# A one-layer hybrid decoder step on one core: where the sampled tokens' state steps stand among the products, and two calls of the output projection's decode rows made one

## The chip, the cores and the metric

The kernel runs on one core of a Trainium2 chip. The metric is the device time of one execution in microseconds (us); three executions of the kernel before took 915.9, 916.09 and 916.25 us, median 916.09 us. The engines are called as in the profile: PE (matrix engine), PEld (its weight loads), DVE (vector), ACT (scalar), POOL and SP (here mostly issuers of DMAs).

## The reference, cut to what matters

One layer of a decoder that joins an RG-LRU group and an mLSTM group of heads. There are two sets of tokens: a prompt of 1,024 new positions, and 8 sampled sequences with one new token each, which carry a state of their own ("decode").

```python
hn = rmsnorm(x, g_norm)
u = hn @ w_in                                    # 1024 -> 7176
xa, za, uq, uk, uv, uo, zb, ui, uf = jnp.split(u, SPLIT_IDX, axis=-1)
yA, hA, bufA = rglru_branch(xa, ...)
hB, C, n, m = mlstm_seq(q, k, v, ig, lf, C0, n0, m0)   # 4 heads, DK = DV = 256
merged = concat([yA * silu(za), norm(sigmoid(uo) * hB) * g * silu(zb)])   # 2048 wide
x = x + merged @ w_out                           # 2048 -> 1024
# inside mlstm_seq, for a sampled token (chunk length 1):
num   = P @ v + ginter * (q @ C)
C_new = carry_scale * C + decay * k v^T          # 256 x 256, per sequence and head
```

For the 8 sampled tokens and 4 heads that is 32 matrices `C` of 256 x 256 floats, which are read, scaled, given a rank-one update, written back and multiplied by a query.

## The kernel before, in words

**The products of the input projection.** `w_in` is taken in 15 *units* of two 256-column blocks each (`UNITS`: v0v1, x0y0, q0k0, ..., z2z3). A unit is worked as 7 products (`Q_P1` to `Q_P7`, in the order `RQ`), each of half the size in every dimension, with sums of operands ahead and sums of results behind. A product has two halves, so a unit has 14 *parts*. A half is a run of triples of full 128x128 matmuls on PE (`mm3`, L66 to L68: high times high, low times high, high times low), 24 of them per half, into one accumulator. What PE reads is split into a high and a low piece first, by ACT (L72) and DVE (L73). DVE takes finished halves out of the accumulators (`evac`, L325 to L362).

**The decode rows of a unit.** The 8 sampled tokens go through the same block of `w_in` in `dec_unit` (L249 to L270): 8 matmuls with a stationary tile of only 32 columns (L256), four side by side in the array. `preps` emits it just behind a unit's last part, so it stands between two units' products on PE. Four transposes (L264) turn the result later.

**The decode steps.** `decode_steps(h)` (L973 to L1028) gives the state steps of head `h`. `first` makes the scaled key and the query tiles and fetches the value row of token 0 (`fetch_v`, L965, an SP queue's DMA into `vbc`). `token(b)` scales the loaded state `Cb` on ACT (L992), adds the rank-one update on DVE (two instructions, L994), stores the state (L996), fetches the next value row and, for even tokens, two more states (`fetch_C`, L971; four buffers `Cb`). For each odd token `products` (L1013) follows two pops later on the list `late`: a *burst* of 4 matmuls with a stationary tile of 4 columns (32 for a head's first burst), 256 wide, over the two states just made. There are 16 bursts in all. The first burst of a head reads `qfirst`, the others `qsel`.

**What sets their places.** Behind every part of a product the main loop (L1690 on) calls `pop_bg` (L712): first it runs what is on `late`, then one entry each of three queues: `bg` (single steps), `rgq` (the RG-LRU group) and `dcq` (the decode steps). `dcq` is popped only on some parts: `DEC = 10, 2, 3` says every third part in units below 10 and every second from unit 10. `first` is a step of its own, so a head has 9 steps. Within an engine a scheduler then moves instructions by its own estimate of when operands are ready.

**From the products to the output.** In the last unit `wo_due` (L1645) loads blocks of `w_out` and makes sums of them (L1379) for a second such set of products, the half of the output projection that belongs to the RG-LRU group. `dec_block` (L1359) multiplies the sampled tokens' rows by those blocks: 8 matmuls of 32 columns for each of two calls (L1368). From there on the tail loop (L1737) takes the prompt's mLSTM chunks and out-projection products in turn. The rows 8 to 15 of `w_out` (the mLSTM group's half) meet the sampled tokens in `wo_dec` (L1483, matmuls L1490 with 32 columns), in two calls: four rows at tail step 19 and four at step 21. Each call ends in `dec_put` (L1353): an ACT copy out of the accumulator and a store that adds into memory.

Of the kernel before, what the change touches and what calls it, by code (L numbers as in the profile page):

```python
# [20 lines left out]
NB = 8  # L21
# [21 lines left out]

UNITS = "v0v1 x0y0 q0k0 x1y1 q1k1 x2y2 v2v3 q2k2 x3y3 q3k3 o0o1 o2o3 z0z1 z2z3".split()
NWS, NSTG, LEAD = 6, 7, 2
DEC = 10, 2, 3
RQ = [Q_P1, Q_P2, Q_P5, Q_P6, Q_P7, Q_P4, Q_P3]
NR, NZ = 28, 4

# [2 lines left out]
def hymba_kernel(  # L52
# [7 lines left out]
    V, A, G, TE = nc.vector, nc.scalar, nc.gpsimd, nc.tensor  # L60
# [21 lines left out]
    def ps(tag, shape):  # L82
        return psp.tile(shape, F32, tag=tag, name=f"ps_{tag}", bufs=NBUF.get(tag, 1))
# [136 lines left out]
    late = []  # L220
    lastt = []

    def run_late():
        now = late[:]
        late.clear()
        for f in now:
            f()
# [482 lines left out]

    bg, rgq, dcq = deque(), deque(), deque()

    def pop_bg(n=1, rg=1, dc=1):
        run_late()
        for q, m in ((bg, n), (rgq, rg), (dcq, dc)):
            for _ in range(m):
                if q:
                    q.popleft()()


    fpr = {}
# [251 lines left out]
    def decode_steps(h):  # L973

        p2 = fpr["p"]
        qsel, qfirst, selq = fpr["qsel"], fpr["qfirst"], fpr["selq"]
        st = {}

        def first():
            st["kw"] = kw = p2.tile([P, 2, NB], F32, tag="kw", name="kw")  # L980
            V.tensor_tensor(kw, dk[:, 2 * h:2 * h + 2, :], dW[:, :, h].unsqueeze(1).to_broadcast([P, 2, NB]), op=ALU.mult)
            V.tensor_copy(qsel.rearrange("p k (m r) -> p k m r", r=9)[:, :, :, 0:5:4],
                          dq[:, 2 * h:2 * h + 2, :].rearrange("p k (m r) -> p k m r", r=2))
            V.tensor_copy(qfirst[:, :, :, 0], dq[:, 2 * h:2 * h + 2, 0:2])
            fetch_v(h, 0)

        def token(b):
            i = h * NB + b

            def f():  # L990
                vb_, C = ds_.pop(("v", i)), ds_["C", i]
                A.mul(C, C, dGI[:, b, h:h + 1])  # L992
                for kb in range(2):
                    V.scalar_tensor_tensor(C[:, kb, :], vb_, st["kw"][:, kb, b:b + 1], C[:, kb, :],  # L994
                                           op0=ALU.mult, op1=ALU.add)
                stq(s_C[0, b, h].rearrange("(kb p) v -> p kb v", p=P), C)  # L996
                if b + 1 < NB:
                    fetch_v(h, b + 1)
                if b % 2:
                    late.append(lambda: late.append(products))  # L1000
                else:
                    fetch_C(i + 2)
                    fetch_C(i + 3)


            def products():
                if b == 1:
                    st["pq"] = ps("qp", [P, 512])
                pq = st["pq"]
                for g in range(4):  # L1010
                    bb, kb = b - 1 + g // 2, g % 2
                    q, n = (qfirst[:, kb, bb, :], 32) if b == 1 else (qsel[:, kb, 4 * bb:4 * bb + 4], 4)
                    TE.matmul(pq[32 * g:32 * g + n, 0:256], q, ds_["C", h * NB + bb][:, kb, :], start=b == 1,  # L1013
                              stop=b == NB - 1, skip_group_check=True)
                for bb in (b - 1, b):
                    del ds_["C", h * NB + bb]
                if b == NB - 1:
                    Z = sg([P, 256], "qC")
                    V.tensor_copy(Z, pq[:, 0:256])

                    def turn():
                        pt = pq[:, 256:272].rearrange("p (v b) -> p v b", v=2)
                        for vb in range(2):
                            TE.matmul(pt[:, vb, :], Z[:, vb * P:(vb + 1) * P], selq, start=True, stop=True)
                        V.tensor_copy(dqC[:, 2 * h:2 * h + 2, :], pt)
                    late.append(lambda: late.append(turn))
            return f
        return [first] + [token(b) for b in range(NB)]  # L1028


    def bh(t):
# [304 lines left out]
    oraw = {}  # L1336
# [145 lines left out]
    def wo_dec(ms):  # L1482

        po = ps("tr", [P, 512])
        with tc.manual_schedule(engines={mybir.EngineType.PE}):
            for m in ms:
                md = mAd[:, NB * (m % 8):NB * (m % 8) + 32]
                for half in range(2):
                    g = 2 * (m % 2) + half
                    TE.matmul(po[32 * g:32 * g + 32, :], md, oraw[m][:, half * 512:(half + 1) * 512], start=m < ms[2],  # L1490
                              stop=m >= ms[2], skip_group_check=True)
        dec_put(po, accum_op=ALU.add)

    def wo_split(**at):
# [34 lines left out]
    def tail():  # L1529
        while tails:  # L1530
            tails.pop(0)()
# [114 lines left out]
    def wo_due(q):  # L1646

        step = lambda *ns: bg.extend([lambda n=n: w_step(n) for n in ns])
        if q == 0:
            w_slot(0, 0, 0)  # L1650
            w_slot(1, 0, 1)
        elif q == 1:
            w_slot(1, 1, 2)
        elif q == 2:
            bg.append(lambda: dec_block(0))
            step("s3", Q_P1)
        elif q == 3:
            bg.append(lambda: dec_block(1))
            step("s1", "s2", "s4")
        elif q == 4:  # L1660
            step(Q_P2)
            bg.append(m_open3)
            step(Q_P5)
        elif q == 5:
            step(Q_P6)
            bg.append(lambda: (r_op(0), r_op(1), r_two()))
            step(Q_P7)
# [12 lines left out]
    last_u = len(units) - 1  # L1680
# [10 lines left out]
    part = 0  # L1691
    for n, (u, q) in enumerate(seq):
        preps(n + 1 + LEAD)
        for _ in product(u, q):
            pop_bg(2 if u == 1 or u == last_u else 1, 1, part % DEC[1 if u >= DEC[0] else 2] == 1)
            part += 1
        if u == last_u:
            wo_due(q)
        if q == 6:
            for kind, j in units[u]:  # L1700
                if kind == "x":
                    rg_unit(j)
            for half in range(2):
                if u == max(unit_of["v", 2 * half], unit_of["v", 2 * half + 1], 1):
                    bg.append(lambda half=half: dec_rows(half))
            for h in range(NH):
                if done_h[h] == u:
                    bg.append(lambda h=h: dcq.extend(decode_steps(h)))
            if u == last_u - 1:
                dgen = decode_outputs()  # L1710

                def step():
                    next(dgen, None)
                    run_late()
                state["out"] = [step] * 5 + [m_open2]
        if not state["m"] and u > max(done_h) and not (bg or rgq or dcq or late):
            m_start()
        if u == last_u and q == 0:
            if not state["m"]:
                while bg or rgq or dcq or late:  # L1720
                    pop_bg()
                m_start()
            bg.extend(state["out"])
# [10 lines left out]
    N2 = 18  # L1734
    for n in range(4, N):
        c, h = n // 4, n % 4
        m_a(n)  # L1737
        so_load(n)
        if n > 4:
            m_g(n - 1)  # L1740
            if n > N2 + 3:
                next(dend, None)
        if n == 6:
            mx["gf"] = gf = [sg([P, HT], f"gf{m}") for m in range(2)]
            for m in range(2):
                stq(gf[m], g_final[m * HT:(m + 1) * HT].partition_broadcast(P))
        m_load(n + 2)
        if h == 3 or n == 4:
            z_load(c if h == 3 else 0)
        if h == 0:  # L1750
            m_n(c - 1)
            fill(2 if n < N2 else 1)
            m_k(n + 1)
            fill(1)
            m_b(n)
            fill(1)
        elif h == 1:
            m_zg(c - 1)
            if n == N2 + 3:
                wo_dec((12, 13, 14, 15))  # L1760
            fill(1)
            m_k(n + 1)
            fill(1)
            m_z(c - 1, 0)
            m_b(n)
            fill(1)
            m_z(c - 1, 1)
            if c - 1 == NZ - 1:
                z_back(NZ - 1)
            elif c - 1 >= NZ:  # L1770
                work.extend([out_part(c - 1, half) for half in range(2)])
            fill(n < N2)
        else:
            fill(1)
            if n == N2 + 1:
                wo_dec((8, 9, 10, 11))
            tail()
            m_k(n + 1)
            fill(2 if n < N2 or h == 2 else 1)
            m_b(n)  # L1780
            fill(1)
# [47 lines left out]
```

## Time and profile before

| what | us |
|---|---|
| median of three executions | 916.09 |
| lowest, highest | 915.9, 916.25 |
| span of the profiled execution | 913.5 |
| PE busy | 902.1 (99%) |
| DVE busy | 741.5 (81%) |
| ACT busy | 590.1 (65%) |
| POOL busy | 194.2 (21%) |

The span is what the profiler saw between the first and the last instruction of one execution. It is 2.6 us less than the median of the executions without a profiler; what lies around the span is taken as unchanged below. Busy shares are means over the span. A matmul's row in the timeline gives its start and the time until its result is out; consecutive matmuls overlap, so the distance from start to start is what one costs.

### The profile page before, as it was taken

Reading aid. Unit: us, or ns where it says so; the run is one execution under the profiler, and the core shown is the slowest. Engines: PE = TensorE matmul, PEld = TensorE weight load, DVE = VectorE, ACT = ScalarE, POOL = GpSimd, SP = SyncE. Lnnn points to the kernel's source line nnn. Section 1 sums busy time; section 2 is a strip of 40 time slices with the busy share of each in tenths; the row PEclk is TensorE's granted clock in tenths of the full one; section 3 lists DMA queues with packets and bytes.
Section 4 is the critical chain, followed back from the end, with each engine's and each line's share of the span. In section 5 each row is a group of like instructions: output and inputs, shape, how many; then the busy total and the mean of one; then the engine's idle time right before and its main releaser. Section 6 shows DMA issues by size and latency. Waiting matters only on the chain.

```text
span 913.5 us, 15513 instructions
## 1 busy us (share of the span) xinstructions
PE 902.1 (99%) x5259; PEld 749.2 (82%) x5259; DVE 741.5 (81%) x1532; ACT 590.1 (65%) x1086; POOL 194.2 (21%) x322
## 2 busy tenths in 40 slices
PE   8999999999999999999999999999999999999996
PEld 6897777877787988787789898877788888888886
DVE  6874788978689878789888786679998879888973
ACT  7663446867567776577658786446786568566642
POOL 1111113112312222324332334010111111121120
PEclk9999999999999999999999999999999999999999
DMA  6611457455746566548665747345789889846531
GB/s 202 193 62 46 138 170 243 134 201 186 229 152 212 165 198 198 192 144 265 202 237 167 266 139 243 108 132 188 217 230 260 201 206 300 225 138 183 181 123 68
DMA packets 130488, 167.68 MB, mean 184 GB/s; under 512 B 17596, under 2 KB 98564, under 8 KB 130402
## 3 DMA queue, kind: packets, MB, share of 16 engines
q1 hardware_dynamic: 108790, 103.68, 37.4%
q0 software_dynamic: 21616, 63.02, 21.0%
q8 instruction: 41, 0.67, 0.3%
q14 instruction: 37, 0.30, 0.1%
q10 hardware_dynamic: 4, 0.00, 0.0%
HBM read 108.00 MB, written 62.92 MB: 187 GB/s over the span
## 4 chain that ended last, share of the span: by engine, by line
PE 97%; ACT 1%; DVE 1%; DMA 0%; issue 0%; POOL 0%; ACTq 0%; POOLq 0%
PE ps_o L66 16%; PE ps_o L68 15%; PE ps_o L67 15%; PE ps_kv L66 12%; PE ps_kv L68 11%; PE ps_kv L67 11%; PE ps_o L256 2%; PE ps_s L1195 2%; PE ps_qp L1013 1%; PE ps_s L824 1%; PE ps_tr L824 1%; PE ps_qp L67 1%; PE ps_qp L66 1%; PE ps_qp L68 1%; PE ps_s L1197 1%; PE ps_o L264 1%
## 5 line engine op out<-in xcount | busy, mean ns | idle before, releaser
L72 ACT CAST wh<-raw 128x1024 fp32r<-128x1024 f32 x91 | 95.4, 1049 | 77.9 <-PE ps_o L67 19.3
L73 DVE TENSOR_TENSOR wl<-raw,wh 128x1024 fp32r<-128x1024 f32 x91 | 111.0, 1220 | 34.9 <-ACT wh L72 19.8
L66 PE MATMUL ps_kv<-cb_hi,wh 128*128 128x512 f32 x320 | 127.3, 398 | 0.0
L68 PE MATMUL ps_kv<-cb_hi,wl 128*128 128x512 f32 x320 | 125.3, 392 | 0.0
L67 PE MATMUL ps_kv<-cb_lo,wh 128*128 128x512 f32 x320 | 125.0, 391 | 0.0
L66 PE MATMUL ps_o<-cb_hi,wh 128*128 128x512 f32 x240 | 95.2, 397 | 0.0
L68 PE MATMUL ps_o<-cb_hi,wl 128*128 128x512 f32 x240 | 93.7, 391 | 0.0
L67 PE MATMUL ps_o<-cb_lo,wh 128*128 128x512 f32 x240 | 93.6, 390 | 0.0
L66 PEld LDWEIGHTS ps_kv<-cb_hi,wh 128*128 128x128 f32 x320 | 60.1, 188 | 22.3 <-issue 4.6
L68 PEld LDWEIGHTS ps_kv<-cb_hi,wl 128*128 128x128 f32 x320 | 60.1, 188 | 13.0
L67 PEld LDWEIGHTS ps_kv<-cb_lo,wh 128*128 128x128 f32 x320 | 60.1, 188 | 12.7 <-issue 0.8
L66 PE MATMUL ps_kv<-wh,cb_hi 128*128 128x256 f32 x192 | 55.1, 287 | 0.0
L67 PE MATMUL ps_kv<-wl,cb_hi 128*128 128x256 f32 x192 | 54.4, 283 | 0.0
L68 PE MATMUL ps_kv<-wh,cb_lo 128*128 128x256 f32 x192 | 54.3, 283 | 0.0
L68 PEld LDWEIGHTS ps_o<-cb_hi,wl 128*128 128x128 f32 x240 | 45.1, 188 | 9.9
L66 PEld LDWEIGHTS ps_o<-cb_hi,wh 128*128 128x128 f32 x240 | 45.1, 188 | 9.7 <-issue 0.8
L66 PE MATMUL ps_o<-wo,mh 128*128 128x512 f32 (+1 forms) x136 | 53.0, 390 | 0.0
L67 PEld LDWEIGHTS ps_o<-cb_lo,wh 128*128 128x128 f32 x240 | 45.2, 188 | 8.9
L68 PE MATMUL ps_o<-wo,ml 128*128 128x512 f32 (+1 forms) x136 | 51.7, 380 | 0.0
L67 PE MATMUL ps_o<-wo,mh 128*128 128x512 f32 (+1 forms) x136 | 51.5, 379 | 0.0
L66 PE MATMUL ps_o<-wh,cb_hi 128*128 128x256 f32 x144 | 41.0, 285 | 0.0
L67 PE MATMUL ps_o<-wl,cb_hi 128*128 128x256 f32 x144 | 40.7, 283 | 0.0
(560 smaller groups left out, 2599.8 us busy)
## 6 DMA issues: line engine op xcount, KB each, us to landing
raw<-in_w_in_dram SPq DMA_DIRECT2D x55, 512.0 KB
Cb<-in_state_mlstm_C_dram SPq DMA_DIRECT2D x32, 256.0 KB
out_dram<-Cb POOLq DMA_DIRECT2D x32, 256.0 KB, 4.5
qk<-d_qk SPq DMA_DIRECT2D x32, 256.0 KB
ring<-d_ro SPq DMA_DIRECT2D x26, 256.0 KB
d_qk<-s POOLq DMA_DIRECT2D x24, 256.0 KB, 4.9
d_x<-s POOLq DMA_DIRECT2D x16, 256.0 KB, 2.8
zsr<-d_y SPq DMA_DIRECT2D x16, 256.0 KB
```

Source lines behind the costliest of these rows:

```text
L66: TE.matmul(out, ah, bh, start=first, stop=False, skip_group_check=True)
L67: TE.matmul(out, ah, bl, start=False, stop=False, skip_group_check=True)
L68: TE.matmul(out, al, bh, start=False, stop=last, skip_group_check=True)
L72: a = A.copy(hi, src)
L73: V.tensor_tensor(lo, src, hi.bitcast(F32), op=ALU.subtract)
L256: TE.matmul(pz[32 * g:32 * g + 32, :], hnd[:, NB * k:NB * k + 32], raws[u, k // 4][:, k % 4, :], start=k < 4, stop=k >= 4, skip_group_chec ...
L264: TE.transpose(pt[:, m, :], Z[:, m * P:(m + 1) * P], idF)
L824: TE.matmul(pg, w[:, n, :], st["xx"][n], start=k == 0, stop=k == 1)
L1013: TE.matmul(pq[32 * g:32 * g + n, 0:256], q, ds_["C", h * NB + bb][:, kb, :], start=b == 1, stop=b == NB - 1, skip_group_check=True)
L1195: TE.matmul(S, qk[:, 2 + kb, :], qk[:, kb, :], start=kb == 0, stop=kb == 1)
L1197: TE.transpose(kn[:, kb * P:(kb + 1) * P], qk[:, 2 + kb, :], idF)
```

## The change

1. `DEC` becomes four places in a unit's 14 parts: decode steps are popped behind parts 2, 5, 8 and 11, in all units.
2. `pop_bg` takes what is on `late` first, and with `late_last` runs it behind the queues' entries instead of ahead of them. The main loop sets that at part 13, the last of a unit, so that a burst due there is emitted directly ahead of the next unit's decode rows.
3. `first` and `token(0)` become one step, so a head has 8 steps, two units' worth.
4. `dec_block(0)` and `dec_block(1)` become one entry of `bg`.
5. `wo_dec` handles rows 8 to 15 in one call at tail step 21, with one `dec_put`.

```diff
-DEC = 10, 2, 3
+DEC = 2, 5, 8, 11
...
-    def pop_bg(n=1, rg=1, dc=1):
-        run_late()
+    def pop_bg(n=1, rg=1, dc=1, late_last=False):
+        now = late[:]
+        late.clear()
+        if not late_last:
+            for f in now:
+                f()
         for q, m in ((bg, n), (rgq, rg), (dcq, dc)):
             for _ in range(m):
                 if q:
                     q.popleft()()
+        if late_last:
+            for f in now:
+                f()
...
-        return [first] + [token(b) for b in range(NB)]
+        start = token(0)
+        return [lambda: (first(), start())] + [token(b) for b in range(1, NB)]
...
-                    TE.matmul(po[32 * g:32 * g + 32, :], md, oraw[m][:, half * 512:(half + 1) * 512], start=m < ms[2],
-                              stop=m >= ms[2], skip_group_check=True)
+                    TE.matmul(po[32 * g:32 * g + 32, :], md, oraw[m][:, half * 512:(half + 1) * 512], start=m < 10,
+                              stop=m >= 14, skip_group_check=True)
...
-            bg.append(lambda: dec_block(0))
             step("s3", Q_P1)
         elif q == 3:
-            bg.append(lambda: dec_block(1))
+            bg.append(lambda: (dec_block(0), dec_block(1)))
...
-            pop_bg(2 if u == 1 or u == last_u else 1, 1, part % DEC[1 if u >= DEC[0] else 2] == 1)
+            pop_bg(2 if u == 1 or u == last_u else 1, 1, part % 14 in DEC, part % 14 == 13)
...
-                wo_dec((12, 13, 14, 15))
+                wo_dec(range(8, 16))
...
-            if n == N2 + 1:
-                wo_dec((8, 9, 10, 11))
```

The lines after L712 move down by 7 or 8, so the burst L1013 is L1020 in the changed kernel, L1368 is L1376, L1379 is L1387, L1490 is L1498.

Three places show how the instructions move. The first is PE at the end of a unit, where the decode rows `L256` stand between one unit's last triples and the next unit's first. Before, the burst comes four triples behind them, among triples of the next unit's first product:

```order
L67 MATMUL ps_kv<-cb_lo_188,wh_0_2118 128x512
L68 MATMUL ps_kv<-cb_hi_187,wl_0_2119 128x512
L1013 MATMUL ps_qp<-Cb,qsel 4x256 x4
L66 MATMUL ps_kv<-cb_hi_187,wh_0_2118 128x512
L67 MATMUL ps_kv<-cb_lo_188,wh_0_2118 128x512
```

and in the changed kernel at the same end of a unit:

```order
L68 MATMUL ps_kv<-cb_hi_199,wl_6_2059 128x512
L1020 MATMUL ps_qp<-Cb,qsel 4x256 x4
L256 MATMUL ps_o<-raw_4_1943,hnd 32x512 x4
L256 MATMUL ps_o<-raw_4_2062,hnd 32x512 x4
L66 MATMUL ps_kv<-cb_hi_187,wh_0_2118 128x512
L67 MATMUL ps_kv<-cb_lo_188,wh_0_2118 128x512
```

The burst has moved up against the decode rows. That is so for 8 of the 16 bursts, each head's second and fourth; the other 8 still stand alone among triples.

The second place is DVE at the hand-over from the last unit to the output projection. `s<-s,ps_kv` (L343) takes a half of the last unit's fifth product out of the accumulator, `ws` (L1379) are sums of blocks of `w_out`, `wr1l` the low piece of one of the operands of the next products. Before:

```order
L1379 TENSOR_TENSOR ws_6801<-wc_6632,ws_6717 128x1024
L343 TENSOR_TENSOR s_6651<-s_6651,ps_kv 128x512
L1379 TENSOR_TENSOR ws_6804<-wc_6658,ws_6801 128x1024
L362 SCALAR_TENSOR_TENSOR s_6651<-tz,s_6651 128x512
L1372 COPY mAd<-mBd 128x64
L1379 TENSOR_TENSOR ws_6804<-wc_6658,ws_6801 128x1024
L73 TENSOR_TENSOR wr1l<-wc_6658,wr1h 128x1024
L343 TENSOR_TENSOR s_6685<-s_6685,ps_kv 128x512
L73 TENSOR_TENSOR wr1l<-wc_6658,wr1h 128x1024
```

and in the changed kernel, where `s_6685` is called `s_6666`:

```order
L1387 TENSOR_TENSOR ws_6781<-wc_6521,wc_6612 128x1024
L343 TENSOR_TENSOR s_6666<-s_6666,ps_kv 128x512
L1387 TENSOR_TENSOR ws_6801<-wc_6612,ws_6705 128x1024 x2
L1387 TENSOR_TENSOR ws_6804<-wc_6673,ws_6801 128x1024
L1380 COPY mAd<-mBd 128x64
L1387 TENSOR_TENSOR ws_6804<-wc_6673,ws_6801 128x1024
L362 SCALAR_TENSOR_TENSOR s_6666<-tz,s_6666 128x512
L347 TENSOR_TENSOR s_6703<-s_6703,ps_o 128x512
L73 TENSOR_TENSOR wr1l<-wc_6673,wr1h 128x1024
```

The two passes each of `ws_6801` and `ws_6804`, the copy and the first pass of `wr1l` stood ahead of this half's evacuation and now stand behind it.

The third place is PE where the sampled tokens' rows meet `w_out` in the last unit (`dec_block`). In the changed kernel the second call stands here:

```order
L68 MATMUL ps_o<-cb_hi_197,wl_5_6688 128x512
L66 MATMUL ps_o<-cb_hi_197,wh_5_6687 128x512
L1376 MATMUL ps_tr<-wc_6673,mAd 32x512
L1376 MATMUL ps_tr<-wc_6612,mAd 32x512
L1376 MATMUL ps_tr<-wc_6673,mAd 32x512
L1376 MATMUL ps_tr<-wc_6612,mAd 32x512
```

Although both calls are one entry of the queue, the scheduler leaves 19 full matmuls between the two runs of 8, and the second run now stands behind the end of the half in `ps_kv`, where before it stood inside that half. In the tail all 16 matmuls of `wo_dec` (L1498) stand in one run, where before there were two runs of 8 (L1490).

## The prediction

> **What bounds the kernel now.** I read the page first, for who is busy and for the chain of waits; then PE's waits; then PE's timeline around a burst, since nearly all of the change is about where small matmuls stand; and last the windows at the hand-over from the last unit to the output projection, where the order changes most.
>
> ```profile
> PE 902.1 (99%) x5259; PEld 749.2 (82%) x5259; DVE 741.5 (81%) x1532; ACT 590.1 (65%) x1086; POOL 194.2 (21%) x322
> PE 97%; ACT 1%; DVE 1%; DMA 0%; issue 0%; POOL 0%; ACTq 0%; POOLq 0%
> ```
>
> PE works 902.1 of 913.5 us, and 97% of the chain that ended last is PE. What PE waits for, by the view of its waits, whose two largest rows these are (us in total, times, longest):
>
> ```profile
> PE ps_tr L533 <- POOL ones L116: 1.1, 1, 1.1
> PE ps_o L67 <- DVE w1l L73: 0.9, 1, 0.9
> ```
>
> No row of that view names a burst, a decode step or a state's DMA. So the time is PE's own sequence, and the change is worth what it takes out of that sequence, unless a place where another engine is about to be late gives it back. The windows show one:
>
> ```profile
> 617.00:640.00 23.00, 22.93 (x117) 17.09 (x116) 22.54 (x57) 14.96 (x23) 2.15 (x4) 1.00 0.56 193
> 640.00:660.00 20.00, 20.00 (x96) 15.16 (x95) 19.56 (x27) 15.38 (x24) 2.74 (x5) 1.00 0.72 217
> 660.00:690.00 30.00, 29.31 (x164) 24.82 (x163) 28.74 (x65) 24.43 (x53) 6.78 (x10) 1.00 0.80 225
> ```
>
> The columns are the length, then busy PE, PEld, DVE, ACT and POOL, the granted clock (1.00) and the DMA share. Over the whole span DVE is 81% busy; here it works 22.54 of 23, 19.56 of 20 and 28.74 of 30 us. PE is the bound in this stretch only just: whatever makes PE earlier here meets a DVE that has nothing left.
>
> **The bursts beside the decode rows.** The cost of a burst that stands alone, from PE's timeline (start, time to the result):
>
> ```profile
> 206.33 0.39 PE L67 MATMUL ps_kv<-cb_lo,wh 128*128 128x512 f32 x1
> 206.56 0.39 PE L68 MATMUL ps_kv<-cb_hi,wl 128*128 128x512 f32 x1
> 206.88 0.61 PE L1013 MATMUL ps_qp<-Cb,qsel 128*4 128x256 f32 x8
> 207.43 0.50 PE L66 MATMUL ps_kv<-cb_hi,wh 128*128 128x512 f32 x1
> 207.76 0.39 PE L67 MATMUL ps_kv<-cb_lo,wh 128*128 128x512 f32 x1
> ```
>
> Full matmuls start 0.23 us apart (206.33, 206.56). The burst starts 0.32 behind the last of them, 0.09 more than the pitch: the entry. The first matmul behind it takes 0.33 to the next, 0.10 more: the exit. From 206.56 to 207.76 are 1.20 us, of which two pitches are 0.46, so the burst costs 0.74. The decode rows by the same reading:
>
> ```profile
> 201.72 0.39 PE L68 MATMUL ps_kv<-cb_hi,wl 128*128 128x512 f32 x1
> 202.04 1.92 PE L256 MATMUL ps_o<-raw,hnd 128*32 128x512 f32 x16
> 203.89 0.50 PE L66 MATMUL ps_kv<-cb_hi,wh 128*128 128x512 f32 x1
> 204.24 0.40 PE L67 MATMUL ps_kv<-cb_lo,wh 128*128 128x512 f32 x1
> ```
>
> 2.52 us from 201.72 to 204.24, less 0.46, is 2.06, with an entry of 0.09 and an exit of 0.12. If the two stand together, one entry and one exit go, 0.19 to 0.21, and the wait of the last narrow matmul for the array to clear goes once too. For that the trace has one place where decode rows were split by a full matmul:
>
> ```profile
> 115.20 0.39 PE L68 MATMUL ps_kv<-cb_hi,wl 128*128 128x512 f32 x1
> 115.52 1.06 PE L256 MATMUL ps_o<-raw,hnd 128*32 128x512 f32 x8
> 116.59 0.33 PE L701 MATMUL ps_qp<-idF,stk 128*128 128x128 f32 x1
> 116.85 1.06 PE L256 MATMUL ps_o<-raw,hnd 128*32 128x512 f32 x8
> 117.84 0.50 PE L66 MATMUL ps_kv<-cb_hi,wh 128*128 128x512 f32 x1
> 118.18 0.39 PE L67 MATMUL ps_kv<-cb_lo,wh 128*128 128x512 f32 x1
> ```
>
> Eight records and what follows take 0.99 (116.85 to 117.84), sixteen took 1.85 (202.04 to 203.89), so eight cost 0.86 and the clearing 0.13. Upper end of a merge: 0.09 + 0.10 + 0.13 = 0.32. Lower end: the split version costs 2.98 less 0.46, or 2.52, which is 0.46 over the whole one; if all of the 0.26 from the start of L701 to the next row is L701's own, 0.20 is left. I take 0.29, nearer to the upper end, because that is made of the burst's own rows. That one kind of narrow matmul can follow another without a gap shows here:
>
> ```profile
> 71.65 0.64 PE L579 MATMUL ps_o<-wg,hnd 128*32 128x8 f32 x15
> 72.12 0.63 PE L256 MATMUL ps_tr<-raw,hnd 128*32 128x512 f32 x3
> ```
>
> L256 starts while L579's row is still open. Both are 32 columns wide there; a burst of 4 columns beside rows of 32 is in no row.
>
> What goes the other way: two bursts stand in before directly beside other small matmuls, one of them here, and no longer in the changed kernel.
>
> ```profile
> 342.17 0.61 PE L1013 MATMUL ps_qp<-Cb,qsel 128*4 128x256 f32 x8
> 342.71 0.60 PE L944 MATMUL ps_s<-idF,dqk 128*8 128x128 f32 x4
> ```
>
> L944 comes 0.54 behind the burst's start, as a full matmul did (206.88 to 207.43 is 0.55), so little was saved there: I take off 0.15 for both, half a merge. The sum up to the last unit is 8 x 0.29 - 0.15 = 2.17 us, between 8 x 0.20 - 0.15 = 1.45 and 8 x 0.32 = 2.56.
>
> [...]
>
> **Steps at fixed places, `first` with token 0.** The number of bursts, of ACT scalings and of DVE updates is unchanged, each as long as before; ACT is 65% and DVE 81% busy, which hides them. Head 3 ends a unit later, and the start of the mLSTM part with it; its bursts still end inside the units, ahead of the hand-over where that part's first products come, so I cost it at nothing.
>
> **`wo_dec` as one run.** Two runs of 16 records become one of 32: one merge, 0.29 (0.20 to 0.32). An ACT copy and a store go as well, off the path.
>
> ```profile
> L1490 PE MATMUL ps_tr<-oraw,mAd 128*32 128x512 f32 x32 | 3.8, 598 | 0.0
> L1368 PE MATMUL ps_tr<-wc,mAd 128*32 128x512 f32 x32 | 3.8, 598 | 0.0
> ```
>
> **`dec_block` as one entry** saves nothing, since the two runs stay apart on PE. But the second run (L1368, half of a row that costs as much per record as L256, so 2.06) now stands behind the end of the half in `ps_kv`.
>
> **The hand-over.** On DVE the evacuation of that half (L343) stood behind four L1379 passes, a copy and one L73 pass, which now stand behind it:
>
> ```profile
> 645.62 0.18 DVE L1372 COPY mAd<-mBd 128x64 f32<-128x64 f32 x1
> 645.72 1.22 DVE L1379 TENSOR_TENSOR ws<-wc,ws 128x1024 f32<-128x1024 f32 x1
> 646.86 1.22 DVE L73 TENSOR_TENSOR wr1l<-wc,wr1h 128x1024 fp32r<-128x1024 f32 x1
> 647.99 0.68 DVE L343 TENSOR_TENSOR s<-s,ps_kv 128x512 f32<-128x512 f32 x1
> 648.59 1.22 DVE L73 TENSOR_TENSOR wr1l<-wc,wr1h 128x1024 fp32r<-128x1024 f32 x1
> 650.24 0.69 DVE L347 TENSOR_TENSOR s<-s,ps_o 128x512 f32<-128x512 f32 x1 [0.44 <-PE ps_o L68]
> ```
>
> By start to start a pass is 1.14 and the copy 0.10, together 5 x 1.14 + 0.10 = 5.8 us. So DVE comes to this evacuation at 647.99 - 5.8 = 642.2. PE's last matmul of the half:
>
> ```profile
> 647.07 0.40 PE L68 MATMUL ps_kv<-cb_hi,wl 128*128 128x512 f32 x1
> 674.36 0.39 PE L68 MATMUL ps_o<-wr4h,ro 128*128 128x512 f32 x1
> ```
>
> Its result, at 647.47, comes 2.17 and 2.06 earlier, at 643.24. DVE, which had no wait there, now waits 1.0 us with 5.8 us of work still to do, and that work lies ahead of the piece PE needs at 674.36:
>
> ```profile
> 672.24 0.68 DVE L73 TENSOR_TENSOR ro<-rtwo,ro 128x512 fp32r<-128x512 f32 x1
> 675.66 0.29 DVE L73 TENSOR_TENSOR pl<-pf,ph 128x128 fp32r<-128x128 f32 x1 [0.70 <-ACT ph L72]
> ```
>
> That piece was done at 672.92, 1.44 ahead of its use. Now it is done at 672.92 + 1.04 - 0.44 (the wait at 650.24 goes) = 673.52, or up to 0.56 earlier if all other idle time of DVE in the last window (30 - 28.74 - 0.70) stood ahead of it and goes too; halfway, 673.24. PE would be there at 674.36 - 2.17 = 672.19, and stands about 1.1 us. So about 1.1 of the 2.17 are left behind this place (0.8 to 1.4), and `wo_dec`'s 0.29 is added much later: 1.1 + 0.29, about 1.4 us.
>
> The profiled execution would be 913.5 - 1.4 = 912.1, and with the 2.6 us around it 914.7. The likeliest case's own range is 914.4 (1.36 + 0.32) to 915.1 (0.8 + 0.2).
>
> **The rivals.**
>
> *Nothing is given back.* If DVE reaches the evacuation no earlier than PE, or the scheduler's other moves (triples of later blocks stand ahead of the late one in the new order) fill PE's wait, all of it stays: 2.17 + 0.29 to 2.56 + 0.32, so 913.2 to 913.6; I take 913.4. For it: PE in before waited nowhere for this piece. Against it: DVE's 0.44 and 0.56 us of slack over 50 us.
>
> *A burst of 4 columns beside rows of 32 still clears the array.* Then a merge saves 0.32 less a clearing and a switch, about 0.1, 0.8 us for eight. By the hand-over's sum the half ends at 644.61, DVE waits 2.4 and the piece comes at about 674.6, 0.3 later than its use before. With `wo_dec`'s 0.29 the sum is zero: 916.1. For it: L944 (8 columns) behind a burst comes no sooner than a full matmul. Against it: the row at 72.12.
>
> *Nothing moves together on the chip.* The change doesn't do what it says, and only the hand-over's new order acts: the half ends at 645.41, the piece at about 675.4, 1.0 behind 674.36: about 917.1.
>
> *Slower: the value row is late.* `first` and token 0 are now one step, so the value row is asked for and used in the same step, behind what SP's queue holds. DVE's update waits, and behind it DVE's splits that PE reads. DVE waited for it before, too:
>
> ```profile
> DVE Cb L994 <- DMA vbc<-d_dv: 4.0, 3, 3.5
> 143.48 1.67 DVE L994 SCALAR_TENSOR_TENSOR Cb<-vbc,kw,Cb 128x256 f32<-128x256 f32 x4 [3.52 <-DMA vbc<-d_dv]
> ```
>
> That 3.52 left no wait of PE in its view, so it decides from somewhere above 3.5 us. At 6 us for each of four heads PE would lose 4 x 2.5 = 10, and the time would be about 925. Against it: the scheduler keeps a pair of steps' updates some rows behind the fetch, as before.
>
> **How the numbers follow.** A measurement of this kernel tells 0.2% (1.8 us) from no change, so faster means below 914.3. Chances: the forecast 0.45, nothing given back 0.20, the array cleared all the same 0.20, nothing together 0.05, the late value row 0.08, and 0.02 for mishaps. Faster: 0.20 and the lower two fifths of the forecast's case, 0.38 in all. Slower (above 917.9): the late value row and the upper part of "nothing together", 0.10. The rest is 0.52. The range 913.3 to 916.6 holds the forecast, most of the first rival and all of the second.
>
> **What would show it.** After the change a burst's row should start 0.32 behind the last full matmul at eight unit ends, and L256 follow 0.43 to 0.46 behind the burst's start; 0.54 or more speaks for the rival of the cleared array. The units' part should end about 2.2 us earlier. At the hand-over PE's waits should gain a row for `ro` of about 1 us, and DVE a wait at L343 of about 1 us with the five passes behind it. Without such a row the first rival holds; a wait of PE for `wl`, with DVE waiting for `vbc` ahead of it, would be the slower one. The forecast is wrong if the tail behind 700 us changes by more than `wo_dec`'s 0.3.

## The result, and the profile after

The changed kernel is slower: 926.65 us, median of 6 runs (924.24 to 932.21), against 916.17 of the kernel before (6 runs beside it). The ratio is 1.0116 with a 95% interval of 1.0102 to 1.013. The forecast was 914.7 with a range up to 916.6.

The profiled execution has a span of 925.3 us, 11.8 more than before. Busy times are nearly the same; the page's first line and the chain of waits:

```profile
PE 904.4 (98%) x5259; PEld 753.9 (81%) x5259; DVE 741.4 (80%) x1532; ACT 589.7 (64%) x1084; POOL 194.1 (21%) x321
...
PE 88%; DVE 4%; DMA 4%; ACT 2%; issue 1%; POOL 0%; SPq 0%; DVEq 0%; ACTq 0%; POOLq 0%
```

PE had 97% of the chain and has 88%; DVE, DMA and ACT have come in. What PE waits for (us in total, times, longest):

```profile
PE ps_qp L1310 <- ACT hh L1259: 3.5, 1, 3.5
PE ps_tr L1376 <- DMA wc<-in_w_out_dram: 2.2, 1, 2.2
PE ps_kv L66 <- ACT c L355: 2.2, 2, 1.9
PE ps_o L68 <- DVE ro L73: 1.3, 2, 0.8
```

All four are new or longer. The row for `ro` is the one that the prediction named; the other three it did not. The windows of the hand-over, with one stretch more behind it:

```profile
617.00:640.00 23.00, 23.00 (x116) 18.82 (x115) 22.57 (x61) 13.83 (x25) 1.62 (x3) 1.00 0.57 186
640.00:660.00 20.00, 17.76 (x93) 11.86 (x92) 17.84 (x29) 14.61 (x24) 2.75 (x5) 1.00 0.62 199
660.00:690.00 30.00, 24.93 (x129) 20.55 (x128) 26.17 (x45) 21.90 (x40) 4.74 (x8) 0.97 0.65 192
690.00:700.00 10.00, 9.44 (x43) 7.92 (x42) 6.65 (x18) 3.61 (x11) 0.88 (x1) 0.75 0.72 178
```

PE stands idle for 2.2 us in the second row (none in before) and for 5.1 in the third (0.7 in before), and the granted clock falls to 0.75 in the fourth.

To find where time is lost or won I compare the start of the same PE row in two timelines. The table gives the start in before, and for the other kernels how much later it is, in us. `L256` are the decode rows at the end of a unit (there are 14 units, one for each entry of `UNITS`), `wr0h` the operand of one of the output projection's products; labels are those of the experiments below.

| PE row | before | changed | only_block | open_late | after_gf | changed_gf_nostates | early_only |
|---|---|---|---|---|---|---|---|
| L256 | 381.61 | -1.25 | 0.14 | 0.11 | -1.43 | -0.91 | -1.26 |
| L256 | 425.00 | -0.36 | 0.13 | 0.10 | -0.64 | 1.01 | -0.85 |
| L256 | 469.15 | -0.66 | 0.12 | 0.09 | -0.67 | 0.71 | -0.85 |
| L256 | 516.88 | 2.18 | 0.12 | 0.09 | 1.53 | -0.41 | -0.54 |
| L256 | 611.34 | 0.07 | 0.12 | -1.66 | -0.57 | -2.52 | -0.55 |
| last wr0h | 748.44 | 12.19 | 9.32 | 6.05 | 6.79 | 4.52 | -0.62 |
| last row | 906.24 | 11.81 | 9.37 | 6.05 | 6.46 | 4.19 | -1.01 |

A row says how much is lost only where both kernels have done the same work ahead of it. At 381.61, 516.88 and 611.34 all of them have the same number of bursts behind them (8, 14 and 16). At 425.00 and 469.15 the kernels that have the new places for head 2 (changed, after_gf, changed_gf_nostates) have done one burst more than before, 0.74 us that are no loss. At 611.34 the kernels in which the mLSTM part opens later have done less: 12 matmuls that read `qk` (L1195, in the changed kernel L1203) stand ahead of that row instead of 16, and with this alone, and no merge, open_late is 1.66 early there.

The changed kernel gains 1.25 us up to 381.61. It loses 3.4 between there and 516.88, gains 2.1 up to 611.34, of which the later opening makes about 1.7, and loses 12.1 between 611.34 and 748.44, where these 1.7 come back.

The gain first. A burst against decode rows, on PE:

```profile
201.97 0.39 PE L68 MATMUL ps_kv<-cb_hi,wl 128*128 128x512 f32 x1
202.29 0.62 PE L1020 MATMUL ps_qp<-Cb,qsel 128*4 128x256 f32 x8
202.72 1.90 PE L256 MATMUL ps_o<-raw,hnd 128*32 128x512 f32 x16
204.55 0.50 PE L66 MATMUL ps_kv<-cb_hi,wh 128*128 128x512 f32 x1
204.89 0.39 PE L67 MATMUL ps_kv<-cb_lo,wh 128*128 128x512 f32 x1
```

L256 starts 0.43 behind the burst's start. From 201.97 to 204.89 are 2.92 us, less two pitches 2.46; apart they cost 0.74 + 2.06 = 2.80. A merge saves 0.34.

**The first loss, at 473.** On ACT of the changed kernel, then on DVE, then on PE:

```profile
451.31 0.58 ACT L340 COPY s<-ps_kv 128x512 f32<-128x512 f32 x1
459.25 0.72 ACT L999 ACTIVATE Cb<-Cb,dGI 128x512 f32<-128x512 f32 x1 [7.36 <-DMA Cb<-in_state_mlstm_C_dram]
459.88 0.67 ACT L781 ACTIVATE rg<-ps_s,hb 64x512 f32<-64x512 f32 x1
```

```profile
453.95 0.68 DVE L343 TENSOR_TENSOR s<-s,ps_kv 128x512 f32<-128x512 f32 x1
460.00 0.88 DVE L1001 SCALAR_TENSOR_TENSOR Cb<-vbc,kw,Cb 128x256 f32<-128x256 f32 x2 [5.38 <-ACT Cb L999]
```

```profile
473.48 0.28 PE L68 MATMUL ps_kv<-wh,cb_lo 128*128 128x256 f32 x1
475.68 0.39 PE L66 MATMUL ps_kv<-wh,cb_hi 128*128 128x256 f32 x1 [1.92 <-ACT c L355]
```

ACT stands 7.36 us for a state that SP asked for at 450.6, and the gates (L781) and casts stand behind it; DVE stands 5.38 us for ACT's scaling with its splits behind it. The state is not needed by PE before its burst at 499.68. What is needed, an evacuation by ACT, is 1.92 late 14 us after, and behind PE's wait the granted clock is 0.50 from about 476.5 to 479.9, an estimated 1.7 us more (half of these 3.4). PE's two waits for `c` (2.2) and the clock make 3.9 us; the 3.4 lost between 381.61 and 516.88 are what the merges in that stretch leave of it. Before, ACT's scaling of that state came behind four gate rows and a cast, and waited 1.90:

```profile
462.86 0.72 ACT L992 ACTIVATE Cb<-Cb,dGI 128x512 f32<-128x512 f32 x1 [1.90 <-DMA Cb<-in_state_mlstm_C_dram]
```

The load took about as long in the changed kernel. SP asked for this state at 454.49 in before and at 450.60 in the changed kernel, and ACT had it 8.4 and 8.7 us later. What differs is how much ACT and DVE have to do behind it. How long a wait this place bears is seen in two runs that have the old order here: ACT stood 2.92 us in early_only and 3.38 in only_wodec, and PE then waited 0.24 and 0.69 at the same evacuation, where 1.90 on ACT in before had cost PE nothing. The row of only_wodec:

```profile
464.26 0.72 ACT L992 ACTIVATE Cb<-Cb,dGI 128x512 f32<-128x512 f32 x1 [3.38 <-DMA Cb<-in_state_mlstm_C_dram]
```

**The second loss, the hand-over.** SP asks for the fourth block of `w_out` (`wc01`) in before at

```profile
637.69 0.37 SPq L1343 DMA_DIRECT2D wc<-in_w_out_dram  x1
```

and in the changed kernel at

```profile
643.03 0.45 SPq L1351 DMA_DIRECT2D wc<-in_w_out_dram  x1
```

5.3 us later; PE's second decode block waits 2.2 us for it. Then ACT, in the changed kernel, with the load it stands for (SP):

```profile
685.78 0.62 ACT L72 CAST ro<-ring 128x512 fp32r<-128x512 f32 x1 [4.44 <-DMA ring<-d_ro]
686.31 0.47 ACT L1259 ACTIVATE hh<-ps_qp,gi_t 128x257 f32<-128x257 f32 x1
```

```profile
679.12 2.02 SPq L1437 DMA_DIRECT2D ring<-d_ro  x4
```

The ring load lands 6.66 us after its issue; PE's transposes need the row behind it on ACT. Two loads of the final gain (`gf`) were issued 1.4 us ahead of it, on POOL:

```profile
677.69 1.44 POOL L1753 DMA_DIRECT2D gf<-in_g_final_dram  x2
```

In before they come behind the ring load:

```profile
673.19 1.42 POOL L1746 DMA_DIRECT2D gf<-in_g_final_dram  x2
```

The pair of ring load and cast in before, SP and ACT:

```profile
671.75 1.94 SPq L1429 DMA_DIRECT2D ring<-d_ro  x4
```

```profile
674.81 0.62 ACT L72 CAST ro<-ring 128x512 fp32r<-128x512 f32 x1 [0.36 <-DMA ring<-d_ro]
```

3.06 us from issue to cast. PE's wait of 3.5 us has a price behind it, in the windows of the changed kernel (the column with 1.00 and 0.50 is the granted clock):

```profile
684.00:686.00 2.00, 0.00 (x0) 0.00 (x0) 1.53 (x4) 0.21 (x1) 0.55 (x1) 1.00 0.94 346
686.00:688.00 2.00, 1.17 (x7) 1.07 (x8) 1.19 (x3) 2.00 (x7) 0.00 (x0) 1.00 0.58 216
688.00:690.00 2.00, 2.00 (x8) 1.69 (x7) 0.44 (x1) 1.75 (x4) 0.55 (x1) 0.52 0.28 98
690.00:692.00 2.00, 1.44 (x7) 1.03 (x6) 0.74 (x3) 0.77 (x2) 0.00 (x0) 0.50 0.28 104
692.00:694.00 2.00, 2.00 (x7) 1.63 (x6) 2.00 (x7) 0.00 (x0) 0.23 (x1) 0.50 0.91 271
694.00:696.00 2.00, 2.00 (x15) 1.96 (x14) 0.90 (x4) 1.10 (x3) 0.65 (x1) 0.77 0.67 91
```

PE works again from 687 on, and from 688 to 695 the granted clock is 0.51.

### The profile page after: what moved, and what is told of

It is laid out like the page before. It is cut to its first block, busy times and chain, and to the rows that moved or that the text cites. A ratio compares the mean times of both kernels' runs of the same rounds, so it can differ in the third digit from the quotient of the medians.

```text
span 925.3 us, 15497 instructions
## 1 busy us (share of the span) xinstructions
PE 904.4 (98%) x5259; PEld 753.9 (81%) x5259; DVE 741.4 (80%) x1532; ACT 589.7 (64%) x1084; POOL 194.1 (21%) x321
## 4 chain that ended last, share of the span: by engine, by line
PE 88%; DVE 4%; DMA 4%; ACT 2%; issue 1%; POOL 0%; SPq 0%; DVEq 0%; ACTq 0%; POOLq 0%
PE ps_o L66 14%; PE ps_o L68 14%; PE ps_o L67 14%; PE ps_kv L66 11%; PE ps_kv L68 10%; PE ps_kv L67 10%; PE ps_o L256 2%; PE ps_s L1203 1%; DMA ring<-d_ro 1%; DMA Cb<-in_state_mlstm_C_dram 1%; PE ps_qp L1020 1%; DMA wc<-in_w_out_dram 1%; PE ps_qp L67 1%; PE ps_qp L66 1%; PE ps_qp L68 1%
## 5 line engine op out<-in xcount | busy, mean ns | idle before, releaser
L67 PEld LDWEIGHTS ps_kv<-cb_lo,wh 128*128 128x128 f32 x320 | 60.2, 188 | 12.1
L999 ACT ACTIVATE Cb<-Cb,dGI 128x512 f32<-128x512 f32 x32 | 22.9, 723 | 32.9 <-DMA Cb<-in_state_mlstm_C_dram 30.1
L66 PEld LDWEIGHTS ps_kv<-wh,cb_hi 128*128 128x128 f32 x192 | 37.5, 195 | 6.4 <-ACT c L355 3.3
```

What stands on the lines that cost most here:

```text
L66: TE.matmul(out, ah, bh, start=first, stop=False, skip_group_check=True)
L67: TE.matmul(out, ah, bl, start=False, stop=False, skip_group_check=True)
```

## The experiments

My first theory was one cause: the mLSTM part opens later, so `wc01` is asked for late. Rivals were the fixed places of the steps, and DVE's new order through the single entry of the decode blocks. Ratios are against the kernel before on the same chip, with 95% intervals.

**m_early_nb.** Decode steps behind every second part again from unit 10 on; the decode blocks as two entries:

```
-  part % 14 in DEC
+  part % 14 in DEC if u < 10 else part % 2 == 1
-  bg.append(lambda: (dec_block(0), dec_block(1)))
+  bg.append(lambda: dec_block(0))
+  bg.append(lambda: dec_block(1))
```

> The changed kernel with two things put back: from unit 10 on a decode step behind every second part, as before, so that the mLSTM part opens as early as before and the fourth block of w_out (wc01) stands at its old place in SP's queue; and the two decode blocks of w_out as two entries. Seven bursts still stand against decode rows. Theory late load (wc01 is issued 5.3 us later behind the mLSTM part's loads, which costs the hand-over about 9 us): the load is issued at about 637 again, no wait of PE for wc, and the time is 913.5 to 915.0. Rival fixed places (the steps at parts 2, 5, 8, 11 make ACT and DVE wait for state loads, and that carries most of the loss): about 918 or more, since the places up to unit 10 are kept. Rival order of DVE (only the pair of decode blocks counts): 914 as well.

Measured: 928.79 us, ratio 1.0146 (1.0131 to 1.0162). My theory of one cause fell. From 611 us to the end this run loses nothing (9.45 and 9.66 late), but 10 us are lost between 469 and 565, on waits such as

```profile
PE ps_kv L66 <- ACT c L353: 3.5, 1, 3.5
```

So there are two losses, and this run cannot speak on the hand-over, because a PE that comes 9 us late gives all others time.

**no_block.** The changed kernel with the decode blocks as two entries.

> The changed kernel with the two decode blocks of w_out as two entries again; all else as changed. Theory late load: the mLSTM part still opens late, wc01 still stands behind a vt, a W, a qk and a ring load on SP, only one qk less; it is issued at about 640 to 642, and the time stays at 920 to 926. Rival order of DVE (the pair of decode blocks puts five passes behind the evacuation, and that is the loss): 914 to 917.

925.46 us, ratio 1.0103 (1.0083 to 1.0123): as slow as the changed kernel, so the single entry isn't the whole loss.

**only_block.** The kernel before with the single entry alone.

> The kernel before with only the two decode blocks made one entry. Theory late load: wc01 stands behind one qk load more on SP and is issued some 3 us later (about 641), part of the loss: 917 to 920. Rival order of DVE: the whole loss of the hand-over, 922 to 926. If neither place matters: 916.

922.35 us, ratio 1.0075 (1.0053 to 1.0097): above what the late load gives and at the lower end of what DVE's order gives. The profiled execution was the slowest of the four; the landmarks put all of its 9.4 us at the hand-over, and no wait for `wc01` is among PE's waits, so the late load, which was to explain it, does not. What does, on DVE and ACT of this run (before: 669.37 and 674.81):

```profile
672.58 2.35 DVE L73 TENSOR_TENSOR wr5l<-ws,wr5h 128x1024 fp32r<-128x1024 f32 x2
```

```profile
681.76 0.62 ACT L72 CAST ro<-ring 128x512 fp32r<-128x512 f32 x1 [4.57 <-DMA ring<-d_ro]
```

The passes that moved behind the evacuation make DVE 3.2 us later at `wr5l`. The ring loads are issued when that is done, at 674.96 instead of 671.75, and so behind two loads of the final gain (`gf`, issued on POOL at 673.53) instead of ahead of them. They land 6.8 us after issue. PE stands 3.6 us for it, and the granted clock is 0.76 from 681 to 683 and 0.50 from 683 to 691.

**only_wodec.** The single call for rows 8 to 15 alone.

> The kernel before with only the sampled tokens' rows 8 to 15 of w_out in one call. One run of narrow matmuls less: 0.29 us (0.20 to 0.32) faster by the recorded prediction, 915.8 against 916.1, all else in place; the ratio would be 0.9997.

915.46 us, ratio 0.9996 (0.9988 to 1.0005): as expected in size, not told from no change.

**after_gf, only_block_gf, before_gf.** In each, the only edit is where `gf` is asked for:

```
-  if n == 6:
+  if n == 12:
```

> The changed kernel; only the two loads of the final gain (gf, POOL queue, 2 x 256 KB, first used at about 800) are asked for at tail step 12 instead of 6. The order on PE and DVE is the same. Theory of the collision: DVE's passes, moved behind the evacuation, end 3 us later, so the ring loads are issued behind the gf loads instead of ahead of them, land after 6.7 us instead of 3, ACT's cast stands for them, behind it the scaling that PE waits for, and PE's idle time of 3.5 us costs another 4 us at half the granted clock. Then without gf in the way the ring load lands in 3 to 4.5 us, PE's wait at the transposes of hh falls below 1.5, no stretch at half clock follows, and the time is 916 to 920. Rival (DVE's later end alone carries the loss): 925 to 927.

> The kernel before with the two decode blocks as one entry, and the gf loads at tail step 12. Theory of the collision: of the 6.5 us that the one entry costs by itself 4 to 6 go, 916 to 918. Rival (DVE's later end alone): 922.

> The kernel before with only the gf loads at tail step 12. Theory of the collision: the ring loads stand ahead of gf's there already, so little to win: 915.0 to 916.2. If gf's place is worth something by itself, the two runs beside this one must be read against it.

Changed kernel: 922.76 us, ratio 1.0068 (1.0053 to 1.0083) instead of 1.0116. Single entry: 919.77, ratio 1.0043 (1.0028 to 1.0058) instead of 1.0075, 2.6 us where I had expected 4 to 6; these two intervals overlap a little. Before: 915.94, ratio 0.9999 (0.9989 to 1.0008). The collision is shown on the changed kernel, though its size was overrated: about 4 of its 10.5 us, where I had expected 7 to 11. ACT's wait is halved:

```profile
682.87 0.62 ACT L72 CAST ro<-ring 128x512 fp32r<-128x512 f32 x1 [2.13 <-DMA ring<-d_ro]
```

PE's wait there is 1.1 instead of 3.5, and the granted clock stays 1.00 from 682 to 692.

**m_early_nb_nost.** The first run above, with states not loaded: `G.memset(t, 0.0)` in place of the load for `i >= 20`.

> The kernel of the first group that opens the mLSTM part early (928.8), with the last 12 of the 32 states not loaded but set to zero by POOL: it leaves out 3 MB of state loads, so its sampled tokens' states of two heads are those of a zero start. Theory of the state loads: from 450 us on a state's load lands after 6 to 9 us, and ACT's scaling and DVE's update, which the scheduler put right behind it although PE needs them some 35 us later, stand for it at the head of their queues; without the loads the loss from 450 to 570 us goes, 913.5 to 917. Rival (the order of the RG-LRU work on ACT and DVE is what is late): 924 or more.

922.85 us, ratio 1.0074 (1.0049 to 1.0099). PE is 1.02 early at 516.88 instead of 3.62 late, so the loads are the cause up to there; but 11 us are lost between 517 and 565, on other waits (3.8 for L353, 3.9 for L927, the RG-LRU group's step for the sampled tokens). Half of the expectation holds. What is late behind 517 in that variant I did not pursue; the changed kernel gains there.

**after_gf_nost** (the program of after_gf a second time, nothing left out of it).

> The changed kernel with gf at tail step 12 once more, one look: a second profile of the same program, for how far the places of its waits repeat. Expected: the wait of PE for the evacuation by ACT near 473 (2 us), for wc01 near 648 (2.3) and for the transposes of hh near 683 (1.1) all come back within 0.5 us.

One run, 925.04 us. The waits come back: 1.9 at the evacuation, 2.6 for `wc`, 1.3 for `hh`. The span is 3.3 us more than in after_gf, 2.2 of it at the hand-over up to `wr0h`. One profile of these kernels is good to some 3 us, so the shares below are, too. With it the five runs of this program took 921.8 to 925.0 us, the six of the changed kernel 924.2 to 932.2: the gain from a later `gf` stands, its size is rough.

**no_block_gf.** Two entries and late `gf`.

> The changed kernel with the two decode blocks as two entries and the gf loads at tail step 12. Theory of the collision: the run with two entries and early gf (ratio 1.0103) showed no stretch at half clock behind 680, so later gf loads bring little here, at most 2 us: 922 to 925. Rival (whatever is late, gf makes it 4 us later): 920 to 921.5.

922.95 us, ratio 1.0078 (1.0062 to 1.0094): inside the first expectation, with the interval overlapping that of no_block. In no_block ACT waits 0.72 us for the ring loads, which come 2.7 us behind `gf`'s there (682.07 against 679.38), so there is little left for a later `gf` to win. After_gf and no_block_gf end alike (1.0068 and 1.0078): once `gf` is out of the way, the entries make no difference that these runs tell. The single entry by itself loses only where the late opening hasn't already cost as much (only_block).

**early_only.** New places and the joined step for heads 0 and 1 only, and the decode blocks as two entries:

```
-  part % 14 in DEC, part % 14 == 13
+  part % 14 in DEC if u < 9 else part % LATE[1 if u >= LATE[0] else 2] == 1, u < 9 and part % 14 == 13
+  if h > 1: return [first] + [token(b) for b in range(NB)]
```

> The new places of the decode steps and the joined first step for heads 0 and 1 only (units below 9), the old ones from unit 9 on; the two decode blocks as two entries; rows 8 to 15 of w_out in one call. Four bursts stand against decode rows; from unit 9 on PE and DVE have the order of the kernel before. Theory (merging is worth 0.3 us a burst, and the loss comes from what the other places do on ACT, DVE and SP from unit 9 on): 4 x 0.29 + 0.29 less the two lost neighbours is 1.3 us faster, 914.2 to 915.2, ratio 0.9985. Rival (the new places cost in the early units, too): 916 or more.

915.72 us, ratio 0.9994 (0.9984 to 1.0004); the profiled span is 912.4, 1.1 less than before. It lies between the two forecasts (914.2 to 915.2, and 916 or more) and decides between neither. It has four merges and `wo_dec`, and no new wait of PE above 0.4. With only_wodec it is the fastest of the versions, and neither is told from the kernel before.

**after_gf_out.** The decode outputs at the head of the queue in the last unit: `bg.extendleft(reversed(state["out"]))` in place of `bg.extend`.

> The changed kernel, gf at tail step 12, and the five steps of the decode outputs with the opening of the wc01 buffer put ahead of what is left of the mLSTM part's first steps on the queue, so that wc01 is asked for earlier. Theory of the late load: PE's wait of 2.3 us for wc01 goes or halves, and DVE's passes of wr5 end 2 us earlier: 919.5 to 922 against 922.8 with gf alone. Rival (wc01 is only a place at which a late PE is seen): no change, 922 to 924.

925.48 us, ratio 1.0099 (1.0071 to 1.0128): no help, and above both ranges. `wc01` was asked for at 643.38, as late as ever, because the buffer it goes to is freed by a store of the decode outputs, and that was issued at 640.65 here and at 640.20 in the changed kernel, 635.75 in before. The edit didn't move what it was to move, so it decides nothing.

**open_late.** The kernel before; the mLSTM part opens one product later, and nothing else is touched:

```
-  if not state["m"] and u > max(done_h) and not (bg or rgq or dcq or late):
+  if not state["m"] and (u, q) >= (12, 0) and not (bg or rgq or dcq or late):
```

> The kernel before, and only the opening of the mLSTM part comes one product later (not before the first product of unit 12 is done), as the changed kernel has it; no burst, no decode step and no decode block is moved. Theory of the late opening: the part's loads and the decode outputs come one step later on SP, POOL and DVE, wc01 is asked for some 4 to 6 us later, and the hand-over costs 5 to 7 us: 920 to 923. Rival (the hand-over's loss comes from the one entry for the two decode blocks and from PE's being earlier, not from the opening): 916 to 917.5.

922.75 us, ratio 1.0078 (1.0056 to 1.0099). The opening suffices: the landmarks show -1.66 at 611 and 6.05 at 748. PE's new waits in this run:

```profile
PE ps_tr L1368 <- DMA wc<-in_w_out_dram: 1.4, 1, 1.4
PE ps_kv L66 <- DVE Cf L1256: 1.3, 1, 1.3
```

`wc01` is asked for at 643.58, as late as in the changed kernel. PE waits 1.4 us for it. The rest of the 6 us is in other late things and in PE's clock: from 676 to 680 PE works only 1.56 of the 4 us, no wait being longer than 1.3, and from 680 to 684 the granted clock is 0.57.

**changed_gf_nostates.** after_gf without the loads of the last 12 states.

> The changed kernel with gf at tail step 12, and the last 12 of the 32 states set to zero by POOL instead of loaded: it leaves out 3 MB of state loads, so the sampled tokens' states and outputs of two heads are those of a zero start. Theory of the state loads: ACT no longer stands 7 us for a state at 459, DVE no longer 5 us behind it, the evacuation near 473 is in time, and PE's wait of 1.9 us there goes: 919.5 to 921, against 922.8 of the same kernel with its loads; the hand-over stays as slow as it was. Rival (the RG-LRU work of that unit is late by itself): the wait near 473 stays, 922 to 924.

919.11 us, ratio 1.0033 (1.002 to 1.0046), against 1.0068 with the loads. PE has no gap near 473:

```profile
470.00:480.00 10.00, 10.00 (x90) 8.57 (x79) 9.52 (x18) 5.10 (x9) 7.08 (x11) 1.00 0.57 187
```

The edit takes away the loads' traffic together with the wait for them; that the wait is what counts rests on the rows of the first loss, where the load took about as long as in before (8.7 us against 8.4). At 611.34 this run is 2.52 us early, but that isn't the merges' worth: 1.7 of it is the later opening, and on the other side PE lost 1.2 at 398.62, in a wait for DVE. The hand-over stays slow, as expected.

## Why the prediction was wrong

- **A merge: right.** 0.29 was taken, 0.34 measured; a burst of 4 columns and rows of 32 stand together without a gap: L256 starts 0.43 behind the burst's start, while the burst's row is still open (202.72 against 202.91), where in before a full matmul came 0.55 behind it (206.88 to 207.43). So the rival of the cleared array is out. The forecast's 0.13 for the clearing was my estimate from the lengths of rows; what PE does in that time no run shows, nor in the switch of that rival's sum, which is the 0.09 or 0.10 of an entry or an exit. At 381.61, with four merges behind it and all of the losses still ahead, the changed kernel is 1.25 us early, early_only 1.26 and after_gf 1.43, where the forecast's terms give 4 x 0.29 less at most 0.15, 1.0 to 1.2. The 2.17 for all eight can't be read off by itself: the losses stand among the last four merges, and the later opening moves the row at 611.34.
- **`wo_dec`: right, as far as it can be told.** 0.29 forecast; from 748 to the end the changed kernel gains 0.38 and early_only 0.39, and the kernel with that edit alone has a ratio of 0.9996.
- **"Head 3 ends a unit later, and the start of the mLSTM part with it; ... so I cost it at nothing": this is the step that failed.** I asked whether the last burst comes before the hand-over, and not what the part's opening puts on the queues. Alone it costs 6 to 7 us (open_late). The opening's loads, the decode outputs and `wc01` stand in one line on SP, POOL and DVE, and all of them move.
- **The hand-over: right place, wrong size, half of the mechanism.** The 5.8 us of DVE work did move, and PE waited for `ro`, 1.3 us against 1.1; but in two places, 0.46 at the one named (`wr4h`, at 679.74) and 0.84 at 671.40, so that the sum agrees is luck. DVE had no wait at L343: the late decode outputs stood ahead of it, and it came there at 647.29, not at 642.2. And I followed DVE's work to PE only, not to the DMA that its end releases. That the ring loads come right behind `gf` costs about 4 us more (shown by moving `gf` in the changed kernel): a wait of 4.4 on ACT, of 3.5 on PE, and the clock of 0.51 from 688 to 695.
- **The slower rival: right mechanism, wrong transfer.** The value row did little (DVE waited for it 5.0 us in total, 2.5 at most). The state did what I had described for it: an update that nobody needs yet stands at the head of a queue until its load has landed. Its threshold of 3.5 us, an estimate from one row of before, is not contradicted: DVE's 5.38 is above it, and PE waited. That the 925 it named is near the 926.65 measured is luck, since its sum was of four waits for the value row. I gave this 0.08 because I looked only at the new step's own fetch.
- **The account of 11.8 us in the profiled execution.** Four merges up to 381.61: -1.25. From there to 516.88, the state loads with some merges: +3.4. Up to 611.34: -2.1, of which about 1.7 is work of the mLSTM part that only moves behind that row. The hand-over: +12.1, in which that 1.7 comes back; about 6 net are the late opening (open_late at 748.44, 6.05) and about 5 the collision (12.1, less the 7.4 that after_gf loses in the same stretch). `wo_dec`: -0.38. The stretches add up to 11.8 by the way they are read; how the hand-over is shared out is good to the 3 us by which two profiles of one program differ.
- **Open:** which of the late things at the hand-over comes first, `wc01` or the decode outputs ahead of it; the only try to move them apart failed.

## What to carry to other kernels

With PE 99% busy, savings of 0.34 us a merge were worth here only as much as the other queues let through: 1.25 us were won up to 381.61, and the end came 11.8 us later. Before pricing such a saving, list every step whose place in program order shifts with the edit, and follow each to the loads that it releases, not only to the instruction that reads its result. An early, unneeded step that stands behind a load, ahead of needed work on the same engine, is a trap. When ACT stood 1.90 us for a state (before), PE waited for nothing at the evacuation behind it; with 2.92 us PE waited 0.24 (early_only), with 3.38 it waited 0.69 (only_wodec), and with 7.36 it waited 1.92 (changed). Where loads that are needed late can come ahead of loads that an engine is about to stand for, ask for them later: with `gf` six steps later the ring load of the changed kernel was cast 4.35 us after its issue instead of 6.66, and the kernel before lost nothing that can be told (ratio 0.9999).

## What the runs showed of the hardware

A lowered clock was a second price of a PE wait. Behind 3.46 us of waiting PE ran at a granted clock of 0.51 from 688 to 695 in the changed kernel: full matmuls start 0.43 us apart there (688.38, 688.81) instead of 0.23. PE is busy for 6.4 of these 7 us, so an estimated 3 us, half of that, are lost. A wait of only 1.92 us was followed by a stretch at half clock, too, in the changed kernel:

```profile
477.00:478.00 1.00, 1.00 (x7) 1.00 (x6) 1.00 (x1) 0.00 (x0) 1.00 (x2) 0.50 0.92 333
```

and in after_gf the same wait (1.93) was not: the clock was 1.00 from 470 to 480. Nor was the wait of 2.24 for `wc` in the changed kernel, with 1.00 from 640 to 660. In open_late three waits of 0.8, 1.3 and 0.6 us close together were followed by 0.57 over 4 us. So in these runs the length of a single wait does not tell whether the clock falls behind it; what does, they do not show.

The same ring loads were cast 3.1 us after issue in before and 6.7 in the changed kernel, from the same queue; in the second, the two loads of `gf` had been issued 1.4 us ahead (677.69 on POOL). In after_gf, without them, it is 4.35 (678.52 to 682.87).
